# Two transformer-like blocks on one core: another byte alignment of the split parts, norm factors one product later, lower halves last, 64-row scores by turns

## The chip, the cores and the metric

One core of one Trainium2 chip. The time is the device time of one launch in microseconds (us): before, the median of three runs is 2158.34 (2155.3 to 2161.16). TensorE multiplies (PE in the rows; PEld is its load of the stationary operand), VectorE (DVE) and ScalarE (ACT) do the element work, GpSimd (POOL) a little set-up, and SyncE (SP) issues the DMAs of the weights.

## The reference

256 tokens of width 1024, all in float32. The first block runs twice: a mixer (retention and a gated delta rule), then a feed-forward net (layer 0) or a choice of 2 of 8 experts (layer 1), then a gated term from per-layer inputs. After a norm the second block runs twice: a mixer of three kinds of heads (mlstm, differential attention, hgrn) and a feed-forward net of width 4096.

```python
def rmsnorm(x, g):
    y = x32 * lax.rsqrt(jnp.mean(x32 * x32, axis=-1, keepdims=True) + EPS)
    return (y * g.astype(jnp.float32)).astype(x.dtype)

def swiglu(x, wg, wu, wd):
    return (jax.nn.silu(x @ wg) * (x @ wu)) @ wd

# hgrn, one chunk of 64 tokens
    diff = Bc[..., :, None, :] - Bc[..., None, :, :]
    decay = jnp.exp(jnp.where(causal, diff, NEG_BIG))
    A = jnp.einsum('bhtk,bhsk,bhtsk->bhts', qb, kb, decay)
# differential attention
    s = jnp.einsum('bhcqd,bhckd->bhcqk', qi, kt)
    p = jax.nn.softmax(jnp.where(mask, s, NEG_BIG), axis=-1)
    a = p[:, :, 0] - lam * p[:, :, 1]
```

## The kernel before, in words

Precision comes from splitting. A float32 operand becomes an upper part (rounded to the matmul's faster float format) and a lower part (what is left), and a product is three matmuls: upper x upper, upper x lower, lower x upper. Activations live transposed, channels on the partitions: `uhi`, `ulo` of 8 slices of 128 channels by 256 tokens.

Weights come in pieces of 1 MB by SP's DMA into `wraw` (two buffers). `piece` splits a piece into two halves of four slices each: ScalarE writes the upper part (L230, `whi`), VectorE the lower (L231, `wlo`); there are four `whi` and four `wlo` buffers, so a piece holds two of each until its product ends. The buffers are 1040 words per partition, one behind the other.

Three product forms matter. `gemm_tok` (L251) takes the activations as the stationary operand and 256, 258, 352 or more weight columns as the moving one; `gemm_b` is its caller. `gemm_a` (L296) and `down_T` (L779) take 128 weight columns as stationary and 256 tokens as moving. With `wave` the first product after a norm goes through the slices in the order in which they become ready: upper, lower, and the third product slice by slice.

A norm isn't applied ahead of the product. `norm_T` makes `uhi` (L433) and `ulo` (L434) from the unscaled hidden state `hT` and the gain; `norm_twice` does it for two norms in a row (L475, L476). The factor of each token comes later: `by_token` (L421) sums the squares with a matmul, `rsqrt` (L343 to L354) is a row of small VectorE instructions, and `along_tokens` (L459 to L461) spreads the factors along the tokens: VectorE puts them on a diagonal `dg`, a matmul with ones (L460) fills a bank, ScalarE copies it to `rsT`. Whoever reads a product's bank multiplies by `rsT`. `norm_twice` also updates `hT` itself with such a factor, eight instructions (L492).

The ffn has 11 iterations: a gate product, an up product, SiLU and product of both, and a down product one iteration later. The second-type mixer (`_second`) walks a list of steps. The hgrn scores are 8 levels per layer (L1694), after one pair at L1668, the mlstm scores four heads (L1758, L1759), the attention scores four heads in two halves (L1809, L1811) with a mask added by a further matmul (L1810, L1812). All have a contraction of 64, that is one half of the partitions: 0 to 63 or 64 to 127. A bank (`bank`) is one of four tagged `acc` or four tagged `sm`.

The order of the program is what the code says only within limits: a scheduler with a timeline of its own reorders each engine's instructions, and each engine then runs its own in that order.

Of the kernel before, what the change touches and what calls it, by code (L numbers as in the profile page):

```python
# [150 lines left out]
class Kernel:  # L151
    def __init__(self, ctx, tc, A, out):
# [3 lines left out]
        self.wp = p("w", bufs=2)  # L156
        self.up = p("u", bufs=2)
        self.hp = p("h", bufs=1)
# [42 lines left out]
    def piece(self, w, k0, c0, pool=None):  # L201
# [52 lines left out]
    def gemm_b(self, x, w, c0, cb, width=256, n=2, tt=False, wave=None, mid=None):  # L254
# [30 lines left out]
    def gemm_a(self, x, wt, ps, wave=False, js=None):  # L285
# [5 lines left out]
        order = [(n, j, i) for n in range(2) for j in js for i in range(3)]  # L291
        if wave:
            order = sorted(order, key=lambda q: q[1])
        for n, j, i in order:
            a, b = parts[i]
            self.nc.tensor.matmul(ps[:, n * 256:(n + 1) * 256], a[j][:, n * 128:(n + 1) * 128], b[:, j, :],  # L296
                                  start=(n, j, i) == (0, 0, 0), stop=(n, j, i) == (1, N - 1, 2))
# [166 lines left out]
    def norm_twice(self, n0, n1, rs):  # L464
# [14 lines left out]

        def fin():  # L480
# [7 lines left out]
            rs.extend(r01[:, t:t + 1] for t in range(2))  # L488
            rT = self.along_tokens([r0[:, t:t + 1] for t in range(2)], name="r0T")
# [4 lines left out]
        return u, fin  # L494
# [367 lines left out]
    def ffn(self):  # L862
        nc = self.nc
        with self.tc.tile_pool(name="pl0", bufs=1) as self.pp, self.tc.tile_pool(name="ffn", bufs=2) as self.mp:
            rs = []
# [7 lines left out]
            down, last = None, []  # L873
            for i in range(11):
                ps = []
                for w in ("ffn_w_gate", "ffn_w_up"):
# [3 lines left out]
                    if down:  # L880
                        down()
                        down = None
                if i == 0:
                    fin()
                    rsT = self.along_tokens(rs)
                g = self.t2("g")
                nc.vector.tensor_tensor(g.rearrange("p (n t) -> p n t", n=2), ps[0].rearrange("p (n t) -> p n t", n=2),
                                        rsT[:, None, :].to_broadcast([128, 2, T]), OP.mult)
                nc.scalar.activation(g, g, AF.Silu)
                nc.vector.tensor_tensor(g, g, ps[1], OP.mult)  # L890
                hi = self.mp.tile([128, 2, T], F32R, name="hhi", bufs=3)
                lo = self.mp.tile([128, 2, T], F32R, name="hlo", bufs=3)
                g3 = g.rearrange("p (k n) -> p k n", k=2)
                nc.scalar.activation(hi, g3, AF.Copy)
                nc.vector.tensor_tensor(lo, g3, hi, OP.subtract)
                x = Split(hi, lo)
                if i < 10:
                    down = lambda i=i, x=x: self.down_T(x, self.piece("ffn_w_down", 2 * i, 0), acc, i == 0, False)
# [20 lines left out]
    def _moe(self):  # L919
# [17 lines left out]
        lg, lT = one([128, 2, 8], "lg"), one([8, T], "lT")  # L937
# [76 lines left out]
    def experts(self, uk, pos, ghl, rhl, s):  # L1014
# [6 lines left out]
        for e0 in range(0, 8, 2):  # L1021
            xe, gs, PT = x
            out = []
            for e in range(2):
                hh = mp.tile([128, 1408], F32, name="hh", bufs=1)
# [371 lines left out]
    def _second(self, l):  # L1397
# [8 lines left out]
        if self.two_norms:  # L1406
            u, fin = self.norm_twice("norm_final", f"norm1_g_2.{l}", rs)
            self.two_norms = False
        else:
            u, fin = self.norm_T(f"norm1_g_2.{l}", rs)  # L1410
        if l == 0:
# [34 lines left out]
        def g_hqf():  # L1446
# [156 lines left out]
        for step in SECOND[l].split():  # L1603
# [50 lines left out]
    def hgrn_scores(self, hT, S2):  # L1654
# [8 lines left out]
        nc.vector.tensor_tensor(E3[:, :, 128:256], E3[:, :, 128:256], q3[:, :, 128:256], OP.mult)  # L1663
        for pa in range(2):
            ps = self.bank("sm")
            rs = slice(pa * 64, pa * 64 + 64)
            for ct in range(2):
                nc.tensor.matmul(ps[:, ct * 128:(ct + 1) * 128], E3[rs, ct, 0:128], E3[rs, ct, 128:256], start=True, stop=True)  # L1668
            nc.scalar.activation(S2[:, pa], ps[:, 0:256].rearrange("p (c i) -> p c i", c=2), AF.Copy)
# [3 lines left out]
        for i, b in enumerate((64, 32, 16, 8, 4, 2, 1, 0)):  # L1673
# [14 lines left out]
            mask = c["levels"][:, i * 64:i * 64 + n].bitcast(I32)  # L1688
            for pa in range(2):
                ps = self.bank("sm")  # L1690
                rs = slice(pa * 64, pa * 64 + 64)
                for j in range(4):
                    js = slice(j * 128, (j + 1) * 128)
                    nc.tensor.matmul(ps[:, j * n:(j + 1) * n], A[rs, js], half(E[rs, js]) if b else fq[rs, js], start=True,  # L1694
                                     stop=True)
# [294 lines left out]
```

## Time and profile before

| what | value |
|---|---|
| median of the runs | 2158.34 us |
| profiled execution | 2161.2 us, span 2159.4 us |
| mean granted TensorE clock | 0.964 of 2.4 GHz |
| TensorE busy | 2078.5 us, 96% |
| VectorE busy | 1546.7 us, 72% |
| ScalarE busy | 1209.9 us, 56% |
| DMA | 403 MB, mean 187 GB/s |

A matmul's busy time includes its way through the array: consecutive ones overlap, so the pace is read from start to start. A granted clock of 0.5 is 1.2 GHz and 1.0 is 2.4 GHz; a mean between says how a stretch is divided. The stages lie in time as: first mixer of layer 0 to 340 us, ffn to 552, gated term to 579, mixer of layer 1 to 909, experts to 1384, gated term to 1413, second-type mixer to 1602, its feed-forward net (ffn2) to 1784, mixer to 1973, ffn2 to the end.

### The profile page before, as it was taken

What the parts mean: (1) busy time and instruction counts of PE and PEld (TensorE: products, weight loads), DVE (VectorE), ACT (ScalarE), POOL (GpSimd) and SP (SyncE); (2) the same over time, 40 slices, a digit from 0 to 9 for tenths busy, and PEclk for the clock granted to TensorE, in tenths of its full rate; (3) what the DMA queues carried; (4) which work ended last, traced back from release to release, by engine and by line L of the source; (5) the groups of instructions that cost most, each with busy time, mean ns of one, the idle gap of its engine ahead of it and who ended that gap; (6) DMA issues with size and microseconds to landing.
All of it is one profiled execution on the core that took longest, in us unless ns stands there. A gap on an engine that the chain in (4) does not pass through costs nothing.

```text
span 2159.4 us, 38877 instructions
## 1 busy us (share of the span) xinstructions
PE 2078.5 (96%) x15686; PEld 1988.7 (92%) x15686; DVE 1546.7 (72%) x2837; ACT 1209.9 (56%) x1799; POOL 35.6 (2%) x89
## 2 busy tenths in 40 slices
PE   7999999999899999989999999889999998999999
PEld 7999999999899999979999898789899998889988
DVE  5789576455767996768889798788765457776444
ACT  5554445444564544458777777665545555555553
POOL 0000000000000000000000000020000002000000
PEclk9999999999999999989999999989789998989999
DMA  5454435455445453539999899643235554323553
GB/s 215 157 176 160 135 137 183 164 187 195 157 153 172 162 167 106 190 121 325 330 323 327 315 334 348 235 152 118 79 113 180 180 192 147 108 78 136 177 195 137
DMA packets 81260, 403.05 MB, mean 187 GB/s; under 512 B 25232, under 2 KB 25392, under 8 KB 45360
## 3 DMA queue, kind: packets, MB, share of 16 engines
q1 hardware_dynamic: 61056, 391.66, 50.9%
q10 hardware_dynamic: 17888, 4.39, 1.0%
q0 software_dynamic: 2128, 4.43, 0.8%
q8 instruction: 125, 2.05, 0.4%
q14 instruction: 63, 0.52, 0.1%
HBM read 398.35 MB, written 2.10 MB: 185 GB/s over the span
## 4 chain that ended last, share of the span: by engine, by line
PE 41%; DMA 6%; DVE 4%; ACT 2%; issue 1%; POOL 0%; ACTq 0%; DVEq 0%
PE acc L251 17%; PE sm L296 8%; PE acc L779 6%; DVE wlo L231 3%; PE acc L296 2%; DMA xraw<-in_exp_w_gate 2%; ACT whi L230 2%; PE sm L1694 1%; DMA xraw<-in_exp_w_down 1%; DMA xraw<-in_exp_w_up 1%; DMA wraw<-in_exp_w_up 1%; PE sm L1094 1%; PE sm L1811 1%; PE sm L1065 0%; PE sm L312 0%
## 5 line engine op out<-in xcount | busy, mean ns | idle before, releaser
L231 DVE TENSOR_TENSOR wlo<-wraw,whi 128x1024 fp32r<-128x1024 f32 (+3 forms) x646 | 737.7, 1155 | 376.5 <-ACT whi L230 363.4
L230 ACT ACTIVATE whi<-wraw 128x1024 fp32r<-128x1024 f32 (+3 forms) x646 | 637.0, 1005 | 571.8 <-PE acc L251 190.8
L251 PE MATMUL acc<-whi,uhi 128*128 128x256 f32 (+3 forms) x1920 | 556.9, 301 | 9.0 <-ACT whi L230 3.6
L251 PE MATMUL acc<-whi,ulo 128*128 128x256 f32 (+3 forms) x1920 | 556.1, 300 | 7.3 <-DVE ulo L434 4.4
L251 PE MATMUL acc<-wlo,uhi 128*128 128x256 f32 (+3 forms) x1920 | 549.7, 301 | 2.5 <-DVE wlo L231 2.2
L251 PEld LDWEIGHTS acc<-whi,uhi 128*128 128x128 f32 x1920 | 364.7, 194 | 13.4 <-ACT whi L230 6.3
L251 PEld LDWEIGHTS acc<-whi,ulo 128*128 128x128 f32 x1920 | 365.0, 194 | 8.7 <-DVE ulo L434 4.8
L251 PEld LDWEIGHTS acc<-wlo,uhi 128*128 128x128 f32 x1920 | 363.1, 194 | 8.0 <-DVE wlo L231 7.1
L296 PE MATMUL sm<-uhi,wlo 128*128 128x256 f32 x864 | 242.6, 281 | 0.9 <-DVE wlo L231 0.9
L296 PE MATMUL sm<-uhi,whi 128*128 128x256 f32 x864 | 242.4, 281 | 0.1
L296 PE MATMUL sm<-ulo,whi 128*128 128x256 f32 x864 | 242.3, 281 | 0.0
L296 PE MATMUL acc<-ulo,whi 128*128 128x256 f32 x704 | 201.6, 287 | 5.1 <-DVE ulo L434 3.7
L296 PE MATMUL acc<-uhi,wlo 128*128 128x256 f32 x704 | 200.7, 286 | 0.8 <-DVE wlo L231 0.8
L296 PE MATMUL acc<-uhi,whi 128*128 128x256 f32 x704 | 200.4, 286 | 1.0 <-ACT uhi L433 0.9
L231 DVE TENSOR_TENSOR wlo<-xraw,whi 128x704 fp32r<-128x704 f32 (+1 forms) x174 | 163.9, 978 | 35.7 <-ACT whi L230 34.0
L230 ACT ACTIVATE whi<-xraw 128x704 fp32r<-128x704 f32 (+1 forms) x174 | 142.7, 861 | 48.9 <-PE acc L251 17.7
L296 PEld LDWEIGHTS sm<-uhi,wlo 128*128 128x128 f32 x864 | 163.6, 189 | 1.8 <-DVE wlo L231 1.7
L296 PEld LDWEIGHTS sm<-uhi,whi 128*128 128x128 f32 x864 | 164.0, 190 | 1.0 <-ACT whi L230 0.4
L296 PEld LDWEIGHTS sm<-ulo,whi 128*128 128x128 f32 x864 | 163.5, 189 | 0.7 <-DVE ulo L434 0.2
L296 PEld LDWEIGHTS acc<-ulo,whi 128*128 128x128 f32 x704 | 135.5, 193 | 6.5 <-DVE ulo L434 4.6
L296 PEld LDWEIGHTS acc<-uhi,whi 128*128 128x128 f32 x704 | 135.4, 193 | 1.8 <-ACT uhi L433 1.1
L296 PEld LDWEIGHTS acc<-uhi,wlo 128*128 128x128 f32 x704 | 135.7, 193 | 1.0 <-DVE wlo L231 1.0
(651 smaller groups left out, 3361.8 us busy)
## 6 DMA issues: line engine op xcount, KB each, us to landing
wraw<-in_w_in SPq DMA_DIRECT2D x80, 1024.0 KB, 4.8
wraw<-in_w_up SPq DMA_DIRECT2D x32, 1024.0 KB, 4.8
wraw<-in_w_down SPq DMA_DIRECT2D x32, 1024.0 KB, 4.8
xraw<-in_exp_w_down SPq DMA_DIRECT2D x24, 1024.0 KB, 7.0
wraw<-in_exp_w_gate SPq DMA_DIRECT2D x32, 704.0 KB, 5.4
xraw<-in_exp_w_up SPq DMA_DIRECT2D x32, 704.0 KB, 5.5
wraw<-in_exp_w_up SPq DMA_DIRECT2D x32, 704.0 KB, 5.7
xraw<-in_exp_w_gate SPq DMA_DIRECT2D x31, 704.0 KB, 5.7
```

What stands on the lines that cost most here:

```text
L230: nc.scalar.activation(hi[:, :mm], raw[:, s], AF.Copy)
L231: nc.vector.tensor_tensor(lo[:, :mm], raw[:, s], hi[:, :mm], OP.subtract)
L251: nc.tensor.matmul(o, a[:, k0 + j, ts], b[j], start=start and i == 0 and j == 0, stop=stop and i == 2 and j == n - 1)
L296: self.nc.tensor.matmul(ps[:, n * 256:(n + 1) * 256], a[j][:, n * 128:(n + 1) * 128], b[:, j, :], start=(n, j, i) == (0, 0, 0), stop=(n, j ...
L779: self.nc.tensor.matmul(o, a[j][:, n * 128:(n + 1) * 128], b[:, k0 + j, :], start=start and n % 2 == 0 and j == 0 and i == 0, stop=stop an ...
L1094: nc.tensor.matmul(pg[:, j * 256:(j + 1) * 256], uk[t][i][:, ks], P[t], start=t == 0, stop=t == 1)
L1694: nc.tensor.matmul(ps[:, j * n:(j + 1) * n], A[rs, js], half(E[rs, js]) if b else fq[rs, js], start=True, stop=True)
L1811: nc.tensor.matmul(ps[:, 128:384], q[:, 128:256], k, start=True, stop=False)
```

## The change

It has four parts. Three small tiles that nothing reads (128, 64 and 192 bytes per partition) and a width of 1088 in place of 1040 words move the byte addresses of the split parts. In the ffn and in the second-type mixers `along_tokens` is called one product later, the `hT` update of `norm_twice` with it. In a first product with `wave` the matmuls with the activations' lower half come last. And the score matmuls of 64 rows are issued with the two halves of the partitions by turns into two banks. Also the router's small `lT` shares a buffer with `hh`.

```diff
@@ Kernel pools
         self.wp = p("w", bufs=2)
+        self.wp.tile([128, 32], F32, name="shiftw", bufs=1)
         self.up = p("u", bufs=2)
+        self.up.tile([128, 16], F32, name="shiftu", bufs=1)
@@ piece
-            hi = self.wp.tile([128, 1040], F32R, name="whi", bufs=4)
-            lo = self.wp.tile([128, 1040], F32R, name="wlo", bufs=4)
+            hi = self.wp.tile([128, 1088], F32R, name="whi", bufs=4)
+            lo = self.wp.tile([128, 1088], F32R, name="wlo", bufs=4)
@@ gemm_b
-            for js in (range(6), range(6, 8)):
-                for t in range(2):
-                    for j in js:
-                        for i in range(n):
-                            self.gemm_tok(x, [p[j:j + 1] for p in wave[i]], ps[t][:, i * width:(i + 1) * width], t, k0=j,
-                                          start=i == 0 and j == 0, stop=i == n - 1 and j == 7)
+            order = [(t, j, i, s) for js in (range(6), range(6, 8)) for t in range(2) for j in js for i in range(n) for s in (0, 2)]
+            order += [(t, j, i, 1) for t in range(2) for j in range(8) for i in range(n)]
+            for t, j, i, s in order:
+                a, b = ((x.hi, 0), (x.lo, 0), (x.hi, 1))[s]
+                self.nc.tensor.matmul(ps[t][:, i * width:(i + 1) * width], a[:, j, t * 128:(t + 1) * 128], wave[i][b][j],
+                                      start=(j, i, s) == (0, 0, 0), stop=(j, i, s) == (7, n - 1, 1))
@@ gemm_a
         if wave:
-            order = sorted(order, key=lambda q: q[1])
+            order = sorted(order, key=lambda q: (q[2] == 1, q[1]))
+            end = order[-1]
@@ norm_twice
+            r0s.append(r0)
+
+        def late():
+            r0, = r0s
             rT = self.along_tokens([r0[:, t:t + 1] for t in range(2)], name="r0T")
@@ ffn
+            self.mp.tile([128, 48], F32, name="shiftf", bufs=1)
...
-                    if down:
+                    if i == 1 and len(ps) == 1:
+                        rsT = self.along_tokens(rs)
+                        use()
+                    elif down:
                         down()
                         down = None
...
                 if i == 0:
                     fin()
-                    rsT = self.along_tokens(rs)
...
+                else:
+                    use()
@@ _second
-            def mid():
-                fin()
-                rsT.append(self.along_tokens(rs))
-
-            self.gemm_b(u, W, 2568, cb, wave=wave, mid=mid)
+            self.gemm_b(u, W, 2568, cb, wave=wave, mid=fin)
...
-        for step in SECOND[l].split():
+        for i, step in enumerate(SECOND[l].split()):
+            if i == 2:
+                rsT.append(self.along_tokens(rs))
+                late()
@@ hgrn_scores
+            two = [self.bank("sm") for _ in range(2)]
+            for j in range(4):
+                js = slice(j * 128, (j + 1) * 128)
+                for pa in range(2):
+                    rs = slice(pa * 64, pa * 64 + 64)
+                    nc.tensor.matmul(two[pa][:, j * n:(j + 1) * n], A[rs, js], half(E[rs, js]) if b else fq[rs, js],
+                                     start=True, stop=True)
             for pa in range(2):
-                ps = self.bank("sm")
-                rs = slice(pa * 64, pa * 64 + 64)
-                for j in range(4):
...
+                ps = two[pa]
@@ attention
+            two = [self.bank("sm") for _ in range(2)]
+            for s, x, y in ((slice(0, 128), slice(0, 128), slice(0, 128)), (slice(128, 384), slice(128, 256), slice(0, 256))):
+                for g in range(2):
+                    gs = slice(g * 64, (g + 1) * 64)
+                    nc.tensor.matmul(two[g][:, s], aT["q"][gs, h, x], aT["k"][gs, h, y], start=s.start == 0, stop=False)
             for g in range(2):
-                gs = slice(g * 64, (g + 1) * 64)
...
+                for s in (slice(0, 128), slice(256, 384)):
+                    nc.tensor.matmul(two[g][:, s], idb, negb, start=False, stop=s.start > 0)
@@ ffn2
+            self.mp.tile([128, 48], F32, name="shiftf", bufs=1)
```

The mlstm scores and the first hgrn pair are reordered in the same way as the hgrn levels.

How the order moves on TensorE. First the ffn, at the end of its second product, where the sums by token (L421, in the new file L425) and the factors along the tokens (L460, new L464) stand; `sm_` with a number is a bank's tile, and `sm_4417` before and `sm_4404` after are the third product. Before:

```order
L296 MATMUL sm_4323<-ulo_4177,whi_4319 128x256
L296 MATMUL sm_4323<-uhi_4176,wlo_4320 128x256
L421 MATMUL sm_4372<-ones_90,t4_4178 128x1 x2
L460 MATMUL sm_4393<-dg_4392,ones_90 128x128
L296 MATMUL sm_4417<-uhi_4176,whi_4409 128x256
L296 MATMUL sm_4417<-ulo_4177,whi_4409 128x256
```

After, at the same place and then 48 matmuls further on:

```order
L300 MATMUL sm_4326<-uhi_4179,wlo_4323 128x256
L425 MATMUL sm_4375<-ones_92,t4_4181 128x1 x2
L300 MATMUL sm_4404<-uhi_4179,whi_4396 128x256
...
L300 MATMUL sm_4404<-uhi_4179,wlo_4401 128x256
L464 MATMUL sm_4455<-dg_4454,ones_92 128x128 x2
L300 MATMUL sm_4479<-uhi_4179,whi_4471 128x256
```

Before, the factors' first matmul stands directly behind the sums; after, a whole product lies between them, and the fourth product begins right behind the factors.

Second, the first product of the first second-type mixer on TensorE (L251 before, L265 after); `acc_` is its bank, `uhi`, `ulo` the activations' halves. Before:

```order
L251 MATMUL acc_20716<-whi_20584,uhi_20602 128x256
L251 MATMUL acc_20717<-whi_20584,uhi_20602 128x256
L251 MATMUL acc_20716<-whi_20584,ulo_20603 128x256
L251 MATMUL acc_20716<-wlo_20585,uhi_20602 128x256
L251 MATMUL acc_20716<-whi_20594,uhi_20602 128x256
L251 MATMUL acc_20716<-whi_20594,ulo_20603 128x256
```

After:

```order
L265 MATMUL acc_20719<-whi_20587,uhi_20605 128x256
L265 MATMUL acc_20719<-wlo_20588,uhi_20605 128x256
L265 MATMUL acc_20719<-whi_20597,uhi_20605 128x256
L265 MATMUL acc_20720<-whi_20587,uhi_20605 128x256
L265 MATMUL acc_20720<-wlo_20588,uhi_20605 128x256
L265 MATMUL acc_20720<-whi_20597,uhi_20605 128x256
```

The third matmul needed the lower half of the activations; now the first ones need only the upper half and both halves of the weights.

Third, the scores in the same mixer on TensorE (hgrn: L1694 before, L1713 after; attention: L1809 and L1811 before, L1833 after), where two `sm_` tiles with neighbouring numbers are the two halves of the partitions. Before:

```order
L1694 MATMUL sm_21649<-E_21638 128x64 x4
L1694 MATMUL sm_21660<-E_21655 128x64 x4
L1694 MATMUL sm_21666<-E_21655 128x64 x4
L1809 MATMUL sm_21679<-ak_21315,aq_20921 128x128
L1810 LDWEIGHTS idb_92
```

After:

```order
L1713 MATMUL sm_21647<-E_21641 128x64 x4
L1713 MATMUL sm_21663<-E_21658 128x64
L1713 MATMUL sm_21664<-E_21658 128x64
...
L1833 MATMUL sm_21682<-ak_21318,aq_20900 128x128
L1833 MATMUL sm_21682<-ak_21318,aq_20900 128x256
L1836 LDWEIGHTS idb_94
...
L300 MATMUL acc_21990<-ulo_20606,whi_21982 128x256
L1833 MATMUL sm_21683<-ak_21318,aq_20900 128x128
L1833 MATMUL sm_21683<-ak_21318,aq_20900 128x256
```

The second level now alternates between its two tiles, the first still has four of one tile in a row, and of the attention head the two halves stand apart, with masks and other products between.

## Rows read from the trace of the kernel before

**Rows 1.** Windows: stretch, its length, busy us per engine, clock, DMA share, GB/s.
```profile
340.00:552.00 212.00, 206.90 (x1760) 206.25 (x1759) 117.80 (x140) 98.08 (x114) 0.00 (x0) 0.99 0.52 180
1413.00:1602.00 189.00, 179.03 (x1249) 166.27 (x1249) 141.06 (x414) 100.82 (x197) 12.96 (x33) 0.85 0.29 102
```
**Rows 2.** Timeline of TensorE in one ffn2 product: start, length, instruction.
```profile
1654.91 0.28 PE L296 MATMUL sm<-uhi,whi 128*128 128x256 f32 x1
1656.33 0.28 PE L296 MATMUL sm<-uhi,whi 128*128 128x256 f32 x1
1659.11 0.28 PE L296 MATMUL sm<-uhi,whi 128*128 128x256 f32 x1
1660.47 0.28 PE L779 MATMUL acc<-hhi,whi 128*128 128x256 f32 x1
```
**Rows 3.** Chain of waits in the same ffn2: start, length, what.
```profile
1643.82 5.56 PE sm L296 x48
1649.38 5.70 PE acc L779 x48
```
**Rows 4.** Grouped instructions of TensorE: busy us, mean ns, idle before, who ended it.
```profile
L251 PE MATMUL acc<-whi,ulo 128*128 128x256 f32 x1088 | 297.8, 292 | 7.3 <-DVE ulo L434 4.4 <-DVE ulo L476 2.9
L296 PE MATMUL sm<-uhi,wlo 128*128 128x256 f32 x864 | 242.6, 281 | 0.9 <-DVE wlo L231 0.9
L296 PE MATMUL acc<-ulo,whi 128*128 128x256 f32 x704 | 201.6, 287 | 5.1 <-DVE ulo L434 3.7 <-DVE ulo L320 1.3
L779 PE MATMUL acc<-hlo,whi 128*128 128x256 f32 x432 | 119.6, 280 | 0.0
```
**Rows 5.** Timeline of TensorE where the factors are spread; [idle before, releaser].
```profile
378.52 0.46 PE L460 MATMUL sm<-dg,ones 128*128 128x128 f32 x2 [4.40 <-DVE dg L459]
379.24 0.42 PE L296 MATMUL sm<-uhi,whi 128*128 128x256 f32 x1
381.80 0.41 PE L296 MATMUL sm<-uhi,whi 128*128 128x256 f32 x1
1448.67 1.22 PE L460 MATMUL sm<-dg,ones 128*128 128x128 f32 x4 [4.02 <-DVE dg L459]
1814.15 1.22 PE L460 MATMUL sm<-dg,ones 128*128 128x128 f32 x4 [7.25 <-DVE dg L459]
```
**Rows 6.** Chain of waits in the other second-type mixer.
```profile
1801.49 7.70 DMA wraw<-in_w_in
```
**Rows 7.** Timelines of ScalarE and TensorE at splits and first products.
```profile
1809.30 2.00 ACT L230 ACTIVATE whi<-wraw 128x1024 fp32r<-128x1024 f32 x2 [6.99 <-DMA wraw<-in_w_in]
...
1418.34 0.58 PE L251 MATMUL acc<-whi,ulo 128*128 128x256 f32 x1 [2.89 <-DVE ulo L476]
1422.92 0.91 ACT L475 ACTIVATE uhi<-hT,g 128x256 fp32r<-128x256 f32 x2 [2.17 <-DVE hT L860]
1431.57 2.01 ACT L230 ACTIVATE whi<-wraw 128x1024 fp32r<-128x1024 f32 x2 [2.22 <-PE acc L251]
```
**Rows 8.** Timeline of TensorE at hgrn scores, and what follows them.
```profile
1501.91 1.00 PE L1694 MATMUL sm<-E 64*128 64x64 f32 x8
1502.85 0.38 PE L296 MATMUL acc<-ulo,whi 128*128 128x256 f32 x1
1509.49 1.60 PE L1694 MATMUL sm<-E 64*128 64x64 f32 x16
1511.03 0.39 PE L296 MATMUL acc<-uhi,whi 128*128 128x256 f32 x1
```
**Rows 9.** Grouped instructions of TensorE in the first second-type mixer, 1413 to 1602.
```profile
L1694 PE MATMUL sm<-E 64*128 64x64 f32 x112 | 13.1, 299 | 0.0
L1811 PE MATMUL sm<-ak,aq 64*128 64x256 f32 x16 | 6.6, 498 | 0.0
L1809 PE MATMUL sm<-ak,aq 64*128 64x128 f32 x16 | 4.2, 347 | 0.0
```
**Rows 10.** Window over most of its scores, columns as in rows 1.
```profile
1500.00:1560.00 60.00, 58.55 (x395) 50.30 (x394) 43.91 (x107) 32.31 (x79) 0.00 (x0) 0.86 0.26 96
```

More of the change, by code (lines that the diff above doesn't have):

```diff
@@ L296, in gemm_a @@
             self.nc.tensor.matmul(ps[:, n * 256:(n + 1) * 256], a[j][:, n * 128:(n + 1) * 128], b[:, j, :],
-                                  start=(n, j, i) == (0, 0, 0), stop=(n, j, i) == (1, N - 1, 2))
+                                  start=(n, j, i) == (0, 0, 0), stop=(n, j, i) == end)
     def new_split(self):
@@ L872, in ffn @@
             acc = [self.bank("acc") for _ in range(4)]
-            down, last = None, []
+            down, last, x = None, [], None
             for i in range(11):
@@ L1410, in _second @@
             u, fin = self.norm_T(f"norm1_g_2.{l}", rs)
+            late = lambda: None
         if l == 0:
@@ L1663, in hgrn_scores @@
         nc.vector.tensor_tensor(E3[:, :, 128:256], E3[:, :, 128:256], q3[:, :, 128:256], OP.mult)
-        for pa in range(2):
-            ps = self.bank("sm")
-            rs = slice(pa * 64, pa * 64 + 64)
-            for ct in range(2):
-                nc.tensor.matmul(ps[:, ct * 128:(ct + 1) * 128], E3[rs, ct, 0:128], E3[rs, ct, 128:256], start=True, stop=True)
-            nc.scalar.activation(S2[:, pa], ps[:, 0:256].rearrange("p (c i) -> p c i", c=2), AF.Copy)
+        ps = [self.bank("sm") for _ in range(2)]
+        for ct in range(2):
+            for pa in range(2):
+                rs = slice(pa * 64, pa * 64 + 64)
+                nc.tensor.matmul(ps[pa][:, ct * 128:(ct + 1) * 128], E3[rs, ct, 0:128], E3[rs, ct, 128:256], start=True, stop=True)
+        for pa in range(2):
+            nc.scalar.activation(S2[:, pa], ps[pa][:, 0:256].rearrange("p (c i) -> p c i", c=2), AF.Copy)
         yield
@@ L1688, in hgrn_scores @@
             mask = c["levels"][:, i * 64:i * 64 + n].bitcast(I32)
-            for pa in range(2):
-                ps = self.bank("sm")
-                rs = slice(pa * 64, pa * 64 + 64)
-                for j in range(4):
-                    js = slice(j * 128, (j + 1) * 128)
-                    nc.tensor.matmul(ps[:, j * n:(j + 1) * n], A[rs, js], half(E[rs, js]) if b else fq[rs, js], start=True,
-                                     stop=True)
+            two = [self.bank("sm") for _ in range(2)]
+            for j in range(4):
+                js = slice(j * 128, (j + 1) * 128)
+                for pa in range(2):
+                    rs = slice(pa * 64, pa * 64 + 64)
+                    nc.tensor.matmul(two[pa][:, j * n:(j + 1) * n], A[rs, js], half(E[rs, js]) if b else fq[rs, js],
+                                     start=True, stop=True)
+            for pa in range(2):
+                ps = two[pa]
                 if b:
@@ L1755, in mlstm_out @@
             pa, ct = h % 2, h // 2
-            rs_ = slice(pa * 64, pa * 64 + 64)
-            ps = self.bank("sm")
-            nc.tensor.matmul(ps[:, 0:256], mT["k"][rs_, ct, 0:128], mT["q"][rs_, ct, :], start=True, stop=True)
-            nc.tensor.matmul(ps[:, 256:384], mT["k"][rs_, ct, 128:256], mT["q"][rs_, ct, 128:256], start=True, stop=True)
-            nc.vector.scalar_tensor_tensor(wm[:, h, :], ps[:, 0:384], 64.0 ** -0.5, wm[:, h, :], op0=OP.mult, op1=OP.mult)
+            if not pa:
+                two = [self.bank("sm") for _ in range(2)]
+                for o, x, y in ((slice(0, 256), slice(0, 128), slice(0, 256)), (slice(256, 384), slice(128, 256), slice(128, 256))):
+                    for i in range(2):
+                        rs_ = slice(i * 64, i * 64 + 64)
+                        nc.tensor.matmul(two[i][:, o], mT["k"][rs_, ct, x], mT["q"][rs_, ct, y], start=True, stop=True)
+                for i in range(2):
+                    nc.vector.scalar_tensor_tensor(wm[:, h + i, :], two[i][:, 0:384], 64.0 ** -0.5, wm[:, h + i, :], op0=OP.mult, op1=OP.mult)
             if pa:
```

46 lines of the change are left out of this document (23 added, 23 removed).

## The prediction

> **What bounds the kernel now.** I read the windows of the stages first, then the timeline and the chain of waits in a stage without stops, then the grouped instructions for counts and waits, and last the timeline where TensorE stops. TensorE is the bound outside the experts: 206.9 of 212 us busy in the ffn and 179.0 of 189 in the first second-type mixer, there at a mean granted clock of 0.85 [rows 1]. So a change is worth what it takes from TensorE's row: its stops, its half-clock stretches (1.2 instead of 2.4 GHz) and its pace.
>
> The pace is not one number. Within one product of the ffn2 of layer 0, 12 matmuls take 1654.91 to 1656.33, 118.3 ns each, and 12 others 1659.11 to 1660.47, 113.3 ns [rows 2]. Between them only the buffer of the weights changes: a piece lies in two. Whole products show both: 48 in 5.56 us (115.8 ns each, half and half) at L296, 48 in 5.70 us (118.8 ns) at L779 [rows 3].
>
> **Part 1, alignment.** A weight buffer is 1040 words, 4160 bytes, 64 more than a multiple of 128, so neighbouring buffers start in alternate 64-byte halves; 1088 words are 17 x 256 bytes, so all start alike. By the allocator's addresses weights then start at 96 and activations at 160, modulo 256: always in opposite halves. By the same addresses the slow 12 of rows 2 have both in one half, the fast 12 in opposite ones; but opposite halves also run at 118 ns for long stretches (half of each L779 product in rows 3 has them). Counts: L296 3 x (864 + 704) = 4704, L779 3 x 432 = 1296, L251 with 256 columns 3 x 1088 = 3264 [rows 4], together 9264, of which I count 8900 at full clock (its mean is 0.85 in the worst stage, 0.99 in the ffn [rows 1]). The mean of rows 3 is 117.3 ns. If all ran at 113.3: 8900 x -4.0 = -36 us. If all stayed at 118.3: +9 us. I take 115.8, the pace of a product that is fast half the time: 8900 x -1.5 = -13 us.
>
> The Trainium skill (TensorE: Matmul & The Clock Gate, Step-by-step: what each phase is for) says that TensorE has two independent read ports, so that loading the next weights takes nothing from the running matmul. By it this part is worth 0. Rows 2 speak against it: the two paces differ with nothing but the buffer.
>
> **Part 2, factors one product later.** L460 puts the norm factors along the tokens and waits for a row of some 15 small VectorE instructions behind L421. In the ffn it waits 4.40 us, then the clock is at half: 379.24 to 381.80 is 12 matmuls, 213 ns each [rows 5], against 118, so 12 x 0.095 = 1.1 us more. Now L421 is followed by a whole product of 48, 5.6 us by rows 3, which covers the 4.40. What is late next: the second up product takes the bank of L460's result and waits for its copy, about one more L460 (0.46 us [rows 5]). Gain 4.40 + 1.1 - 0.5 = 5.0. In the first second-type mixer the wait is 4.02 us [rows 5]; by the new order over 100 matmuls now lie between, and the eight updates of hT that stood in VectorE's queue ahead of the factors move behind them. Gain 4.02 + about 1.1 of clock = 5.1. In the other second-type mixer the stop is 7.25 us, L460 at 1814.15 [rows 5], but the next weights land only at 1801.49 + 7.70 = 1809.19, and ScalarE splits two buffers in 2.00 us from 1809.30 [rows 6, 7]: the first is ready at 1810.3. L460 begins 3.9 us after that and its own 1.22 go too, of which I count 0.9. Gain 4.8. Sum 15 us; bounds 10 (no clock back, a bank wait of 2 us) and 19 (each stop and its clock whole).
>
> On SP's queue one thing moves: the first down piece of the ffn is asked for after the second up piece. VectorE's chain of small instructions has no new instruction queued ahead of it but the next pieces' splits, which it had before.
>
> **Part 3, lower halves last.** Waits on the lower halves sum to 3.7 us at L296 and 4.4 + 2.9 at L251 [rows 4], 11.0 us in all; one of them is 2.89 us long [rows 7]. That is the upper bound before the clock. But the upper halves come late too: ScalarE's last pair at 1422.92 waited 2.17 us for hT [rows 7]; at that time 48 of the 96 matmuls (last two slices, all lower halves) are still due after it. And the next weights' split waits for a buffer that this product frees, 2.22 us at 1431.57 [rows 7]; with every lower half at the end all four buffers are held to the end. I take 4.5 of 11, the rest being given back; bounds 0 and -11.
>
> **Part 4, 64-row scores by turns.** A matmul of float32 shows as two halves. Eight halves on one row group, alone, take 1501.91 to 1502.85, 117 ns each; sixteen on two groups, one behind the other, 1509.49 to 1511.03, 96 ns each, since the second group begins before the first ends [rows 8]. Fully by turns, sixteen would take what eight take now: 0.94 instead of 1.54, 0.6 us saved. In the first of two layers L1694, L1811 and L1809 hold 13.1 + 6.6 + 4.2 = 23.9 us [rows 9]; halved in both layers this is -24, the upper bound. The new order reaches less: of 16 hgrn steps 11 stand by turns (11 x 0.6 = 6.6), 5 still group by group, two of these torn further apart than before; of the attention heads some have both groups adjacent, others, as in the third excerpt of the order, keep other work between. With the mlstm heads I add 4, subtract 1 for the torn ones: 9.6. VectorE reads these banks and is busy 43.91 of 60 us there [rows 10], so a sixth is lost in new waits: -8. Lower bound 0 gain; with two of four score banks taken at once a loss of up to 4 us.
>
> The Trainium skill (TensorEngine Tiling (Array Packing), PSUM Bottleneck) says that after such packing the copies out of the banks may become the bound. VectorE's 73% [rows 10] comes near without reaching it; by that rule alone term 4 would be 0 and the sum -32.
>
> **Sum.** -13 - 15 - 4.5 - 8 = -40.5. The profiled execution took 2161.2 us (span 2159.4), 2.9 above the median of 2158.3, so 2161.2 - 40.5 = 2120.7 there and 2118 on the scale of the medians.
>
> **Rivals.**
> - The pace locks at 118 ns: opposite halves show both paces, and the change takes away the half-and-half products. Term 1 is +9: sum -18.5, 2140. For it: L779's 5.70 us. Against: the 113.3 of rows 2. Chance 0.20.
> - All of it locks at 113.3: term 1 is -36, sum -63, 2095. Chance 0.13.
> - The change doesn't do what it says: the order undoes the turns, and the late upper halves undo part 3. Terms 3 and 4 are 0: sum -28, 2130. For it: the five steps left whole, the 2.17 us of rows 7. Chance 0.12.
> - Slower: in the second-type mixers VectorE, not TensorE, sets the pace of the scores, TensorE stops more often and the clock falls to 1.2 GHz for these whole stretches. In 1500 to 1560 the mean clock is 0.86 [rows 10], so some 72% of it, 43 us, is at full clock and could take twice as long: 86 us over both layers. It decides from 40 of these 86 on; at 60% of them the time is 2118 + 52 = 2170. For it: 0.85 of clock already [rows 1]. Against: TensorE is busy 179 of 189 us there, and its stops get fewer. Chance 0.06.
>
> The forecast has the remaining 0.49, its own range 2108 to 2128. Its neighbours reach from 2095 to 2140; the bounds of parts 2 to 4 add a few us at each end: 2092 to 2148 leaves out the slower case and the ends of the first two rivals. About 0.3%, 6.5 us, is what a measurement can tell from no change. Only the last rival and mishaps of several terms reach it: faster 0.89, within 0.05, slower 0.06.
>
> **What would show it.** Part 1: products of 48 in ffn2 at 5.44 to 5.56 us at both lines; 5.68 or more throughout is the first rival. Part 2: no idle over 1 us ahead of the factors' two matmuls in the ffn and the first second-type mixer, and 3 to 4 us for weights in the other. Part 3: no wait on ulo in a first product, but waits on uhi and a later split. Part 4: sixteen halves in 0.9 to 1.0 us where they stand by turns. The prediction is wrong if the mean clock of the second-type mixers falls under 0.82, or if TensorE waits for score banks.

## The result, and the profile after

The changed kernel takes 2126.0 us (median of 4 runs, 2121.2 to 2130.3) against 2159.5 for the kernel before in the same comparison: ratio 0.9847, 95% interval 0.9821 to 0.9874, that is 33 us less (27 to 39). The profiled execution took 2127.2 us, its span is 2125.3 us, its mean granted clock 0.975. Forecast were 2118 us and a saving of 40.5.

Where the time went, by stages (us, from the end of one stage's last update of `hT` to the next's, worked out from both traces; the mixers are both first-type ones, "second mixers" the two second-type ones):

| stage | before | after |
|---|---|---|
| mixers | 693.3 | 691.2 |
| ffn | 200.1 | 197.0 |
| gated terms | 67.9 | 62.6 |
| experts | 461.6 | 471.2 |
| second mixers | 363.4 | 331.7 |
| both ffn2 | 373.1 | 371.6 |

Nearly all of it is in the second mixers. The windows of after that answer to [rows 1], and in the third line the other second mixer, columns as there:

```profile
341.00:546.00 205.00, 204.14 (x1733) 203.95 (x1733) 116.32 (x138) 96.58 (x111) 0.00 (x0) 1.00 0.52 181
1412.00:1583.00 171.00, 159.23 (x1222) 149.49 (x1223) 136.63 (x408) 97.74 (x190) 12.18 (x33) 0.89 0.33 114
1766.00:1938.00 172.00, 159.43 (x1252) 149.63 (x1251) 137.54 (x397) 97.73 (x189) 16.16 (x35) 0.91 0.34 119
```

The first second mixer needs 159 us of TensorE in place of 179, and its clock rises from 0.85 to 0.89. Much of the gain is clock. Worked out from the granted clock in both traces, the second mixers spend 61 us at half clock in place of 103; a product takes nearly twice as long at half clock (213 ns a matmul against 118 in [rows 5]), so about half of the difference, an estimate of 21 us, is clock, of the 32 saved there. The trace of before had a low clock for its kind: over all runs on record the mean granted clock is 0.969 before (61 runs) and 0.974 in the changed kernel (10 runs), and by the same estimate some 12 of the 33 us are clock.

The chain of waits in the first ffn2, which answers to [rows 3]:

```profile
1618.93 5.65 PE sm L300 x48
...
1630.68 0.22 PE sm L464 x2
1630.90 2.00 PE sm L300 x17
1632.90 0.22 PE sm L464 x2
1633.13 3.52 PE sm L300 x31
1636.65 5.44 PE acc L789 x48
1642.09 5.44 PE sm L300 x48
```

Products of 48 take 5.65 us (117.8 ns each) up to the second pair of factor matmuls, and 5.44 us (113.3 ns) behind it, to the end of the stage. But for the product that the factors interrupt at 1632.90, none here changes its pace inside any more. The timeline of TensorE where the stops of [rows 5] were, and at the first ffn2's first products:

```profile
376.29 0.60 PE L464 MATMUL sm<-dg,ones 128*128 128x128 f32 x4
377.75 0.39 PE L300 MATMUL sm<-uhi,whi 128*128 128x256 f32 x1 [0.86 <-ACT rsT L465]
...
1446.10 0.56 PE L253 MATMUL acc<-whi,uhi 128*128 128x260 f32 x1 [5.71 <-DVE hx L1469]
...
1599.62 0.39 PE L300 MATMUL sm<-uhi,whi 128*128 128x256 f32 x1 [1.86 <-ACT whi L232]
```

In the ffn 0.86 us is left of 4.40. In the first second mixer the wait has not gone but moved: it is 5.71 us, for a bank that `hx` reads with the factors. And a new wait for weights stands in the ffn2. In the other second mixer waits of 2.6 and 1.6 us are left of 7.25. What the 5.71 us wait for is VectorE's row of small instructions from the sums to the factors, with seven splits of weights among them:

```profile
1429.55 0.15 DVE L347 TENSOR_SCALAR rq<-sm 128x2 f32<-128x2 f32 x1
...
1445.01 0.16 DVE L493 TENSOR_TENSOR r<-rq,rt 128x2 f32<-128x2 f32 x1
```

The scores, grouped instructions of the first second mixer (answer to [rows 9]) and the timeline (answer to [rows 8]):

```profile
L1713 PE MATMUL sm<-E 64*128 64x64 f32 x112 | 9.9, 294 | 0.0
L1833 PE MATMUL sm<-ak,aq 64*128 64x128 f32 (+1 forms) x32 | 6.7, 347 | 0.3 <-ACT mix L1866 0.3
```

```profile
1506.55 0.92 PE L1833 MATMUL sm<-ak,aq 64*128 64x128 f32 x4
...
1507.50 0.37 PE L300 MATMUL acc<-uhi,wlo 128*128 128x256 f32 x1
...
1509.08 1.11 PE L1713 MATMUL sm<-E 64*128 64x64 f32 x16
...
1512.44 2.01 PE L1713 MATMUL sm<-E 64*128 64x64 f32 x32
...
1868.46 0.93 PE L1833 MATMUL sm<-ak,aq 64*128 64x128 f32 x8
...
1869.56 0.39 PE L1858 MATMUL sm<-c_base,aa 128*128 128x128 f32 x2
```

23.9 us have become 16.6. Sixteen halves take 1.11 us instead of 1.60, and 32 take 2.01. The row of four is one group (one half of the partitions) of an attention head by itself; the row of eight, in the other second mixer, is both groups of a head, and takes no longer. In the kernel before, a group by itself with the next instruction behind it, and a head with both groups one behind the other:

```profile
1507.61 0.48 PE L1809 MATMUL sm<-ak,aq 64*128 64x128 f32 x2
...
1508.85 0.36 PE L296 MATMUL acc<-uhi,wlo 128*128 128x256 f32 x1
...
1528.84 0.48 PE L1809 MATMUL sm<-ak,aq 64*128 64x128 f32 x2
...
1531.44 0.37 PE L251 MATMUL acc<-wlo,uhi 128*128 128x256 f32 x1
```

With its masks and to the next instruction that head takes 2.60 us, where the row of eight takes 1.10. A group by itself took 1.24 us, with the masks between its scores, and takes 0.95 in the changed kernel (1506.55 to 1507.50), with the masks behind them.

### The profile page after: what moved, and what is told of

Its sections match the earlier page's. It is cut to its first block, busy times and chain, and to the rows that moved or that the text cites. A ratio compares the mean times of both kernels' runs of the same rounds, so it can differ in the third digit from the quotient of the medians.

```text
span 2125.3 us, 38879 instructions
## 1 busy us (share of the span) xinstructions
PE 2039.2 (96%) x15686; PEld 1951.3 (92%) x15686; DVE 1547.2 (73%) x2837; ACT 1210.7 (57%) x1799; POOL 36.6 (2%) x89
## 4 chain that ended last, share of the span: by engine, by line
PE 40%; DMA 7%; DVE 4%; ACT 3%; issue 1%; POOL 0%; ACTq 0%; DVEq 0%
PE acc L253 18%; PE sm L300 8%; PE acc L789 6%; DVE wlo L233 3%; PE acc L300 2%; ACT whi L232 2%; DMA xraw<-in_exp_w_down 2%; DMA wraw<-in_exp_w_gate 1%; DMA wraw<-in_exp_w_up 1%; PE sm L1713 1%; DMA xraw<-in_exp_w_up 1%; PE acc L265 1%; PE sm L1112 1%; PE sm L1083 1%; PE sm L316 0%
## 5 line engine op out<-in xcount | busy, mean ns | idle before, releaser
L253 PE MATMUL acc<-whi,uhi 128*128 128x256 f32 (+3 forms) x1824 | 521.3, 297 | 14.0 <-ACT whi L232 6.7
L253 PE MATMUL acc<-wlo,uhi 128*128 128x256 f32 (+3 forms) x1824 | 515.0, 298 | 6.9 <-DVE wlo L233 4.8
L253 PE MATMUL acc<-whi,ulo 128*128 128x256 f32 (+3 forms) x1824 | 519.8, 296 | 0.0
L253 PEld LDWEIGHTS acc<-whi,uhi 128*128 128x128 f32 x1824 | 339.7, 191 | 19.3 <-ACT whi L232 10.2
L253 PEld LDWEIGHTS acc<-wlo,uhi 128*128 128x128 f32 x1824 | 337.7, 191 | 13.7 <-DVE wlo L233 12.7
L253 PEld LDWEIGHTS acc<-whi,ulo 128*128 128x128 f32 x1824 | 339.8, 191 | 0.7
L300 PE MATMUL sm<-uhi,whi 128*128 128x256 f32 x864 | 240.2, 280 | 3.1 <-ACT whi L232 1.9
L300 PE MATMUL sm<-uhi,wlo 128*128 128x256 f32 x864 | 239.6, 280 | 0.1
L300 PE MATMUL sm<-ulo,whi 128*128 128x256 f32 x864 | 233.6, 279 | 0.0
L300 PE MATMUL acc<-uhi,whi 128*128 128x256 f32 x704 | 198.7, 286 | 4.3 <-ACT uhi L437 2.8
L300 PE MATMUL acc<-uhi,wlo 128*128 128x256 f32 x704 | 199.4, 285 | 0.0
L300 PE MATMUL acc<-ulo,whi 128*128 128x256 f32 x704 | 194.1, 283 | 1.4 <-DVE ulo L324 1.4
L300 PEld LDWEIGHTS sm<-uhi,whi 128*128 128x128 f32 x864 | 162.6, 188 | 4.7 <-ACT whi L232 2.4
L300 PEld LDWEIGHTS sm<-uhi,wlo 128*128 128x128 f32 x864 | 162.7, 188 | 0.6 <-DVE wlo L233 0.5
L300 PEld LDWEIGHTS sm<-ulo,whi 128*128 128x128 f32 x864 | 159.3, 188 | 0.6
L300 PEld LDWEIGHTS acc<-uhi,whi 128*128 128x128 f32 x704 | 134.1, 192 | 5.2 <-ACT uhi L437 3.2
L300 PEld LDWEIGHTS acc<-uhi,wlo 128*128 128x128 f32 x704 | 134.8, 191 | 0.4 <-DVE wlo L233 0.2
L300 PEld LDWEIGHTS acc<-ulo,whi 128*128 128x128 f32 x704 | 131.6, 190 | 1.9 <-DVE ulo L324 1.8
```

The source lines that it names most:

```text
L253: nc.tensor.matmul(o, a[:, k0 + j, ts], b[j], start=start and i == 0 and j == 0, stop=stop and i == 2 and j == n - 1)
```

## The experiments

Theory: four independent terms, of which the alignment sets one of two paces for a whole stretch. The rivals stand in each expectation.

### Each part alone

Each is the kernel before with one part of the change. The kernel before, in the same comparison: 2157.06 us, median of 24 runs, 2145.8 to 2165.3.

**Alignment.**
```diff
+        self.wp.tile([128, 32], F32, name="shiftw", bufs=1)
+        self.up.tile([128, 16], F32, name="shiftu", bufs=1)
-            hi = self.wp.tile([128, 1040], F32R, name="whi", bufs=4)
+            hi = self.wp.tile([128, 1088], F32R, name="whi", bufs=4)
```


> The kernel before with part 1 alone (the three small tiles, the width of 1088, lT in the buffer of hh). Theory (the pace of 256-column matmuls depends on which 64-byte half of 128 bytes the moving and the stationary operand start in, and with opposite halves it settles at about 113.4 or about 117.8 ns for a whole stage): no stretch at 119 to 120 ns is left, each stage lies at one of the two paces, 5 to 13 us faster than before, 2147 to 2155. Rival (alignment is nothing, the reading of the two paces is chance): within 3 us of before and still products of half and half.

Measured: 2156.4 us, ratio 0.9988 (0.9967 to 1.0009), by the ratio 2.6 us saved (-1.9 to 7.1): no change that can be told. But the paces are as the theory has them. Its first ffn2 in the chain of waits, all products at 117.8 ns, where the whole change has them at 113.3:

```profile
1640.72 5.65 PE sm L298 x48
1646.37 5.65 PE acc L781 x48
```

So the gain depends on where each stage settles; over the whole trace the mean is 116.9 ns, against 117.4 before.

**Factors later.**
```diff
-                    rsT = self.along_tokens(rs)
+                    if i == 1 and len(ps) == 1:
+                        rsT = self.along_tokens(rs)
```


> The kernel before with part 2 alone (factors along the tokens one product later, hT updates of the two norms with them). Theory (the three stops ahead of the factors and the half clock behind them go, except 3 to 4 us of weights in the second-type mixer of layer 1): 13 to 17 us faster, 2143 to 2147, with no idle over 1 us ahead of the factors' matmuls. Rival (the stop moves to the bank of the delayed factors or to the next weights): 5 us or less gained.

Measured: 2147.0 us, 0.9950 (0.9935 to 0.9965), 10.8 us saved (7.5 to 14.0): between theory and rival. The ffn gives 5.1 us (200.1 to 195.0), as forecast. TensorE's timeline in the first second mixer, and in the second, where a stop stays:

```profile
1443.55 0.36 PE L251 MATMUL acc<-whi,uhi 128*128 128x260 f32 x1 [1.13 <-ACT whi L230]
...
1807.64 0.56 PE L251 MATMUL acc<-whi,uhi 128*128 128x260 f32 x1 [5.68 <-ACT mv L1503]
```

In the first the stop of 4.02 us is gone, and 1.13 us, for weights, is the longest at this place. In the second, `mv` is the read of a product's bank scaled by the very factor: the matmuls no longer wait for the factors, but soon for a bank that is read only with them. VectorE's row in the first second mixer, with four splits in it:

```profile
1430.59 0.16 DVE L343 TENSOR_SCALAR rq<-sm 128x2 f32<-128x2 f32 x1 [0.16 <-PE sm L421]
...
1442.45 0.16 DVE L489 TENSOR_TENSOR r<-rq,rt 128x2 f32<-128x2 f32 x1
```

**Lower halves last.**
```diff
-            order = sorted(order, key=lambda q: q[1])
+            order = sorted(order, key=lambda q: (q[2] == 1, q[1]))
```


> The kernel before with part 3 alone (lower halves last in first products). Theory (11 us of waits on the lower halves go, more than half is given back to late upper halves and to buffers of the weights held longer): 3 to 6 us faster, 2154 to 2157, waits on the upper halves of 2 us or less in its place. Rival (all of it is given back): within 2 us of before; the other rival (nothing is given back, clock included): 11 to 16 us faster.

Measured: 2158.3 us, 1.0013 (0.9990 to 1.0036): nothing. The gated terms are 7.7 us shorter (67.9 to 60.3), yet new waits stand in the first ffn2 (first line) and in the first second mixer (second line), with their total, number and longest in us:

```profile
PE sm L298 <- ACT whi L230: 1.5, 1, 1.5
PE sm L462 <- DVE dg L461: 6.5, 1, 6.5
```

The stop ahead of the factors in the first second mixer has grown from 4.02 to 6.5 us; in the other, 2.9 and 1.1 us stand in place of 7.25.

**Scores by turns.**
```diff
-            for pa in range(2):
-                ps = self.bank("sm")
+            two = [self.bank("sm") for _ in range(2)]
+            for j in range(4):
+                for pa in range(2):
```


> The kernel before with part 4 alone (64-row scores by turns). Theory (two halves of the array run side by side wherever the order alternates, VectorE takes part of it back): 8 to 12 us faster, 2148 to 2152, all of it in the two second-type mixers, sixteen halves in 0.9 to 1.0 us. Rival 1 (VectorE is the bound there): within 3 us, longer idle of TensorE behind VectorE. Rival 2 (half the clock goes with it, TensorE being busy for less of the time): slower than before, mean clock of these mixers under 0.82.

Measured: 2141.2 us, 0.9923 (0.9896 to 0.9951), 16.6 us saved (10.6 to 22.4): more than the theory. The second mixers shrink from 363.4 to 343.3 us in its trace. Timeline: sixteen halves, and the matmul behind them:

```profile
1520.97 1.11 PE L1695 MATMUL sm<-E 64*128 64x64 f32 x16
1522.01 0.39 PE L296 MATMUL acc<-uhi,whi 128*128 128x256 f32 x1
```

1.04 us for sixteen. The mean clock of the two mixers is 0.87 and 0.88 there, against 0.85 and 0.86: it rose, so rival 2 falls, and the saving is there, so rival 1 falls too. Over its four runs the mean granted clock is 0.973, against 0.969; by the estimate above some 7.5 of the 16.6 us are clock. The part also moves the attention's masks behind the scores, and the two were not run apart.

### The changed kernel with one part changed

The next four share 17 runs of the kernel before (2158.2 us). The first, third and fourth have the same order of instructions on every engine as the changed kernel and differ in addresses alone.

**Without the alignment** (the diff above, undone).

> The changed kernel without part 1 (parts 2, 3 and 4). Theory (the alignment is worth little, since each stage settles at one of two paces, 113.4 or 117.8 ns, on either side of the 117.4 ns that the old addresses give on the mean): 2130 to 2137, 5 to 10 us slower than the changed kernel. Rival (part 1 by itself gave nothing within 4 us, so it gives nothing here): 2123 to 2128.

Measured: 2130.5 us, 0.9885 (0.9849 to 0.9921). The interval, 2126 to 2141 us, holds the theory's range and part of the rival's, and it overlaps that of the changed kernel (0.9821 to 0.9874): not decided.

**Without lower halves last** (the diff above, undone).

> The changed kernel without part 3 (parts 1, 2 and 4). Theory (what the lower halves last save in the gated terms is given back by weight buffers held to the end of the product): within 3 us of the changed kernel, 2123 to 2129. Rival (with the other parts in, part 3 counts as its waits do, 3 to 6 us): 2129 to 2132.

Measured: 2127.9 us, 0.9858 (0.9826 to 0.9889): as the theory has it, part 3 is worth nothing here. Its first ffn2 is 181.4 us, against 184.9 with it, and the wait for `whi` is gone. The waits there, at the bank in the first second mixer, and at one in the other:

```profile
PE sm L298 <- DVE wlo L233: 0.2, 1, 0.2
PE acc L253 <- DVE hx L1467: 0.3, 1, 0.3
PE acc L253 <- ACT mv L1506: 5.9, 1, 5.9
```

So the 5.71 us at `hx` are gone too, and in the other second mixer 5.9 us at `mv` stand in their place.

**All in the same 64-byte half.**
```diff
-        self.up.tile([128, 16], F32, name="shiftu", bufs=1)
```


> The changed kernel without the 64-byte tile ahead of the activations, so that weights and activations of every 256-column product start at 96 bytes modulo 256, in the same 64-byte half. Theory (same half costs): all these products at 119.3 to 119.8 ns, 3 ns above the mean of the changed kernel's trace, over some 9000 matmuls 27 us slower than the changed kernel, about 2153. Rival (the alignment is nothing): 2123 to 2129 with the same two paces.

Measured: 2148.2 us, 0.9957 (0.9938 to 0.9975), 24 us above the changed kernel (17 to 31 by the two intervals), near the 27 forecast. The chain of waits in its first ffn2, both product forms at 120.0 ns:

```profile
1623.83 5.76 PE sm L299 x48
...
1641.96 5.76 PE acc L788 x48
```

Every stage is at 119.5 to 120.0 ns but the experts, whose some 220 matmuls of this width are at 118.1 to 118.7. That 64 bytes in the activations' address count is shown: nothing else differs. That it is the half of 128 bytes, and not the same start modulo 256 alone, the kernel before shows. Sorted by the program's addresses, some 5400 matmuls of its trace up to 1219 us take 119.2 and 118.6 ns on the mean where moving and next stationary operand start 0 and 128 bytes apart (modulo 256), and 116.0 and 114.7 where 64 and 192.

**The other opposite distance.**
```diff
-        self.up.tile([128, 16], F32, name="shiftu", bufs=1)
+        self.up.tile([128, 48], F32, name="shiftu", bufs=1)
```


> The changed kernel with 128 bytes more ahead of the activations, so that they start at 32 modulo 256 and the weights at 96: opposite halves still, but the distance between moving and next stationary operand is 192 in place of 64 bytes for the products of 128 weight columns, and 64 in place of 192 for the others. Theory (only the 64-byte half counts, which of the two paces a stage settles at is chance): the same two paces, other stages fast, 2118 to 2130. Rival (the distance decides: 192 gives the fast pace, as 61 to 64% of the token-major products show in the changed kernel's trace): the ffn and both ffn2 at 113.4 to 115, 15 us faster, about 2110.

Measured: 2120.8 us, 0.9826 (0.9798 to 0.9854). The theory fits: other stages settle fast (the second ffn2 with many products at 5.46 to 5.47 us), the first ffn2 now largely slow; ahead of the changed kernel by less than the intervals.

Mean start-to-start time of the 256-column matmuls at full clock (some 9300 each, worked out from the traces), beside the ratios:

| addresses | mean ns | ratio |
|---|---|---|
| same half | 119.8 | 0.9957 |
| without part 1 | 117.5 | 0.9885 |
| other distance | 116.5 | 0.9826 |
| as changed | 116.3 | 0.9847 |

3.5 ns are worth 24 us, 6.8 us a ns; by the interval of the 24, some 5 to 9.

### What decides between the two paces

**The changed kernel again**, on another chip.

> The changed kernel once more, on the chip of the next two. Theory (which of the two paces a stage settles at follows from the program, by the step at which the stream of matmuls last stopped): the same stages fast and slow as in its first trace: ffn, experts and the second ffn2 at 117.8 ns, the first ffn2 at 113.3 from its second pair of factor matmuls on. Rival (the settling is chance of each execution): other stages fast. The time 2121 to 2131.

Measured: 2129.2 us, 0.9864 (0.9842 to 0.9886). Fast and slow stages are the same, the first ffn2 again fast from its factor matmuls on: the program decides for whole stages, though some short first products differ. Its second mixers take 340.3 us, 8.6 more than in the first trace, with 79 us at half clock against 61: so far apart are two traces of one program.

**One interruption more.**
```diff
+                    if len(ps) == 1 and i in (3, 5, 7, 9):
+                        nc.tensor.matmul(ps[-1][:, 0:128], self.ones, self.ident, start=True, stop=True)
                     self.gemm_a(u, wt, ps[-1], wave=i == 0 and len(ps) == 1)
```


> The changed kernel with one more matmul of 128 columns ahead of the gate product in iterations 3, 5, 7 and 9 of the ffn, into a bank that the product then overwrites; four times some 0.25 us of work. Theory (any such interruption lets the stream settle anew, to 113.3 or 117.8 ns, and it stays there): the pace of the ffn, 117.8 throughout in the changed kernel, changes to 113.3 behind at least one of the four, whole products of 48 in 5.44 us; up to 5 us saved in the ffn. Rival (the pace belongs to the stage, its addresses or its DMA traffic): 117.8 in all of the ffn, 1 us slower.

Measured: 2115.3 us, 0.9801 (0.9778 to 0.9824), 14 us under the run above. Timeline of the ffn, the first and last matmul of the product ahead of the extra one (L891), of the product behind it, and the next:

```profile
403.38 0.28 PE L300 MATMUL sm<-uhi,whi 128*128 128x256 f32 x1
...
409.03 0.38 PE L891 MATMUL sm<-c_base,ones 128*128 128x128 f32 x2
409.17 0.36 PE L300 MATMUL sm<-uhi,whi 128*128 128x256 f32 x1
409.37 0.28 PE L300 MATMUL sm<-ulo,whi 128*128 128x256 f32 x1
...
414.70 0.28 PE L789 MATMUL acc<-hhi,whi 128*128 128x256 f32 x1
```

48 in 5.65 us before it, 47 in 5.33 behind it: 117.7 and 113.4 ns, and 113.3 to the end of the stage. The ffn falls from 197.0 to 192.7 us. That is 4 of the 14 us. Over its runs the mean granted clock is 0.978, against 0.974 in the run above, by the same estimate as before some 8 us. The extra matmuls also made the scheduler move a few hundred of TensorE's other instructions, in the second mixers too, and which of these moves did it was not tried.

### Versions put together

**Chosen.**
```diff
-            order = sorted(order, key=lambda q: (q[2] == 1, q[1]))
+            order = sorted(order, key=lambda q: (q[2] == 1 and wave == 2, q[1]))
```


> A version put together from the runs: parts 2 and 4, the alignment of swap_class, and lower halves last only in the two gated terms and in the second-type mixer of layer 1; the ffn, both ffn2, the mixer of layer 1 and the first second-type mixer keep the old order of their first product. Theory (there the weights' buffers held to the end cost more than the waits on lower halves): the first ffn2 3 to 4 us shorter than in swap_class, the two mixers 2 to 3 us each, 2110 to 2116. Rival (these differences are the spread of single executions): 2118 to 2124, as swap_class.

Measured: 2112.8 us, 0.9778 (0.9755 to 0.9802), as the theory has it and clear of the changed kernel on the same chip (0.9864). By stages, against the trace of swap_class: the first ffn2 is 3.3 us shorter and the second-type mixer of layer 1 2.4; the first second mixer is no shorter (166.4 to 166.2), although its stop of 7.7 us at `hx` is gone. There the theory failed.

**Joined.**

> The version chosen, but with the alignment of the changed kernel in place of that of swap_class, and one extra matmul of 128 columns ahead of the gate product in iteration 3 of the ffn. Theory (the gains of kick and of chosen add: one interruption is enough for the ffn, the first ffn2 settles fast by itself, and shorter stops after the first products): ffn at 192 to 193 us from that product on at 113.3 ns, first ffn2 178 to 182, 2104 to 2112. Rival (the new order moves the step at which streams restart, so other stages settle slow): 2112 to 2120.

Measured: 2111.4 us, 0.9765 (0.9730 to 0.9800): not told apart from the last. Within the theory's time, but its step failed: the extra matmul in the ffn did not settle it fast. Timeline:

```profile
409.29 0.38 PE L893 MATMUL sm<-c_base,ones 128*128 128x128 f32 x2
409.43 0.36 PE L302 MATMUL sm<-uhi,whi 128*128 128x256 f32 x1
409.63 0.28 PE L302 MATMUL sm<-ulo,whi 128*128 128x256 f32 x1
...
415.16 0.28 PE L791 MATMUL acc<-hhi,whi 128*128 128x256 f32 x1
```

47 in 5.53 us, 117.7 ns. The same interruption can lead to either pace; what of its moment decides stays open.

## Why the prediction was right, and where it was not

The time lay in the range and on the right side, in part by luck: part 4 alone gave twice its term, and the other three gave less than theirs. Neither sign of being wrong came: the clock of the second-type mixers is 0.89 and 0.91, and in the first of them the attention scores waited 0.3 us in all for a bank, the hgrn scores not at all. Term by term:

- **Alignment, -13 forecast, nothing told alone** (2.6 us saved, -1.9 to 7.1). The mechanism held: same half 119.8, opposite halves 113.3 or 117.8 ns. The step that failed is the pace of 115.8 for all: the mean came to 116.3. A ns is worth some 5 to 9 us by the runs; the 8.9 that the count of 8900 gave lies at the upper end. At 6.8, (117.4 - 116.3) x 6.8 = 7 us, which the runs with and without part 1 neither show nor exclude. The first rival (the pace locks slow) came true in the ffn and the second ffn2, the second rival in the first ffn2. That a stage would hold one pace throughout was in the rivals, not in the forecast's half-and-half.
- **Factors later, -15 forecast, 10.8 measured alone** (7.5 to 14.0). The ffn's 5 is right, with the bank wait (0.86 us) seen ahead. Two steps failed. The matmuls that "now lie between" take the four `acc` banks, and those are read with the same factors: TensorE waits for a bank instead, 5.68 us at `mv` in the run of this part alone. I followed L460's consumers and not those of the scaled copies. And that VectorE's chain has nothing new ahead of it holds for this part alone, but not with part 3. In the first second mixer the chain takes 12.0 us alone (1430.59 to 1442.62) and the stop of 4.02 us is gone; in the changed kernel seven splits stand in the chain in place of four, it takes 15.6 us (1429.55 to 1445.17), and TensorE waits 5.71 us. The other traces agree: where this mixer has parts 2 and 3 (six traces) that stop is 5.7 to 7.7 us with seven splits, where it has part 2 without part 3 (four traces) at most 1.3 us with four. In the other second mixer it is the reverse: 5.7 and 5.9 us at `mv` without part 3, no wait over 2.6 there with it.
- **Lower halves last, -4.5 forecast, nothing measured** (+2.8, -2.2 to +7.8). At the lower bound that was stated. The traces show what it gives and takes: the gated terms get 7.7 us shorter, the stop in one second mixer goes and the one in the other grows. The reason stated, buffers held to the end, fits a wait of 1.5 to 1.9 us for `whi` in the first ffn2 with half clock behind it, gone without part 3. It is not the only condition: that wait is absent with part 3 in both in the version with the extra matmuls and in the one with all in the same half, which has the very order of the changed kernel. What decides stays open.
- **Scores by turns, -8 forecast, 16.6 measured alone** (10.6 to 22.4). Two steps failed. The term put the clock at nothing, and by the estimate above that is some 7.5 us. And I counted little for the attention heads, where the two groups stand one behind the other: with the masks moved behind, both groups of a head take 0.93 us, as long as one by itself, and the whole head 1.10 in place of 2.60. A single group gains too, 1.24 to 0.95, so part of this is the masks' move and not the turns. For the sixth taken off for VectorE no wait is seen.

The four terms measured alone add to 27 us, the whole change saves 33 (27 to 39): the totals show no interplay, though the stop in the first second mixer is one of parts 2 and 3. The experts' 9.6 us more are not traced to a part: the changed kernel's other trace has 468.8, and of all traces here the kernel before's 461.6 is the shortest (to 471.2), with the same instructions there except for a shared buffer; the median landing of `in_exp_w_down` is 7.0 us in the one and 7.4 in the other. The kernel before has only one trace, so how much of the 9.6 is its spread is not known.

The sentence of the Trainium skill (TensorE: Matmul & The Clock Gate, Step-by-step: what each phase is for), by which loading the next weights takes nothing from the running matmul, does not fit the addresses here: 24 us between two kernels that differ in addresses alone. That the load is what takes the time is a reading; no run separates it from the matmul's own operand. The other sentence of the Trainium skill (TensorEngine Tiling (Array Packing), PSUM Bottleneck), which speaks of a fourfold speed-up, was not reached: the copies out of the banks did not become the bound, as the 0.3 us above show.

## What to carry to other kernels

Where a wait for a factor is pushed back, look for every reader that needs the same factor, above all those that free banks; the wait ends at the first of them. A change of order also moves what stands in the queue of the engine that makes the factor. A stream of equal matmuls has to be read from start to start, product by product: a mean over a stage hides two paces and a switch between them. And one trace against another is good to about 10 us, in the DMA-bound experts and in the second mixers, where the clock differs from run to run; a term of that size is settled by runs of the part alone, with their granted clocks beside the times.

## What the runs showed that was not expected

- A stream of 256-column matmuls has three paces at full clock: 119.8 ns with both operands in the same 64-byte half of 128 bytes, 113.3 or 117.8 ns in opposite halves. In opposite halves it keeps its pace over more than 1000 matmuls. It changes it at an interruption, as at 1632.90 in the changed kernel or at 409.03 with the extra matmul, or where one product form follows another without one, as at 70.78, 635.98 and 781.78 in the changed kernel, each time from 117.8 at L300 to 113.3 at L253.
- Two row groups overlap even without turns: the second starts when the first has about four halves left (at 1510.00 in the sixteen of [rows 8]), so turns save some 0.5 us of 1.54 per sixteen halves, not half.
- The same program spreads over 0.9% from run to run: 2145.8 to 2165.3 us in 24 runs of the kernel before on one chip, three times the 0.3% that the forecast took as the limit of what can be told.
